# Layer 3 of a diffusion backbone: the gate product's operands without the norm's factor, and a rewritten last stage

## The chip, the cores and the metric

One core of a Trainium2 chip runs the whole program in a single launch. The metric is the device time of one execution in microseconds (us). Before the change three runs took 2101.03 us in the median (2100.48 to 2101.74).

## The reference, cut to what matters

A stack of four layers runs over 256 latent tokens and 256 context tokens of width 2048. Each layer computes RMSNorm, a shift and scale from a conditioning vector, a mixer with a SiLU gate, an output projection, and a gated residual. Layer 0 and layer 3 mix with a Fourier transform, layer 1 is an mLSTM, layer 2 is attention. In layer 3 only the latent tokens are left.

```python
shift, scale, gate = jnp.split(sc @ ada_w[i] + ada_b[i], 3, axis=-1)
hx = _rmsnorm(x, norm_g[i]) * (1.0 + scale[:, None]) + shift[:, None]
# layers 0 and 3
y = (_fourier_mix(hx) * jax.nn.silu(hx @ w_gate)) @ w_out
x = x + gate[:, None] * y
# after the last layer
return _rmsnorm(x, final_g)          # x * rsqrt(mean(x*x) + EPS) * final_g
```

RMSNorm multiplies each token by one number, rstd = 1 / sqrt(mean(x*x) + EPS). Written with a per-token rstd and a per-feature scale s = norm_g * (1 + scale), the gate product of layer 3 is hx @ w = rstd * ((x * s) @ w) + shift @ w.

## The kernel before, in words

**Layout and products.** Activations stand feature by token: a tile of 128 features by 512 tokens (256 context columns, then 256 latent columns), 16 tiles for the 2048 features, numbered kt. A product is done in fp32r in three parts: an operand x is held as h (rounded to fp32r) and l (the rest, x - h), a weight as wh and wl, and the product is h*wh + h*wl + l*wh. For each kt there are two SBUF tiles, with the tags h0 to h15 and l0 to l15, made by hl_pair (L364) and filled by split_into (L369) or modulate (L401). Each is allocated anew for each use, which waits for the readers of the tile that had the place before.

**gemm** (L276) does one group of 512 output features, in 8 steps k2 of two kt each. With orientation "A" the weights are stationary, the activation streams (columns t0 to t1), and four banks of PSUM collect 128 features each. With "B" the activation is stationary and the banks are token blocks of 128. A weight pair for one k2 comes from next_w and make_w (L258): a DMA of 512 KB into wraw (four buffers), an ACT cast to wh (L267), a DVE subtraction to wl (L268), each with three buffers. The last steps of a group, the tail (two k2 steps, if not said otherwise), run bank by bank, and done(b, ps) is called after each bank's last matmul, to take the bank out. With first=True the earlier steps run kt by kt over all the banks, otherwise bank by bank. gemm is a generator that yields every few matmuls; it yields "made" when the weights of the tail and one pair of the next group are made. run() steps it and, at given rates per yield, steps three queues of other work: fill (the mixers), bg (the conditioning) and adq.

**Order.** TensorE's (PE's) instructions run in the order in which the program emits them. For the other engines a planner sets the order, from the dependencies and its own costs: an instruction can stand earlier in an engine's queue than in the program, if what it reads is there. Where the program doesn't want that, it ties an instruction behind another.

**Conditioning.** ada (L76) holds shift, scale and gate of all layers. Their products with ada_w are made in the background by ada_dve (L212): DMA loads and DVE multiplications, 8 steps per chunk, queued in bg under the keys ga0, l1, ga1, l2, ga2, l3, ga3 (L735 to L739). bg.finish(key) runs the queue up to that key. A bias tile adab (L74) is loaded once (L615) and added in ada_finish (L164). In the first 120 us, layer 0's own conditioning is made on PE; there land_l (L180) uses the places of not yet needed l tiles as landing places, with two loads of 256 KB for a pair.

**Around the change.** out_proj (L445) is called for layer 2 at L1275: four groups "A" over 256 columns, each bank evicted by done (L458): rn = bank * gate + old residual on DVE (L467), a square on ACT (L473), its sum on DVE (L474). Then, at L1277 to L1310: bg.finish("l3"); turn_x (L1282) transposes rn into token-major xtk, on PE with ACT copies; rstd_cols (L377) sums the squares with four matmuls against ones (L383), takes the root on ACT and the reciprocal on DVE; rstd_rows (L392) spreads rstd along the tokens by two transposes of diagonals; then modulate(3, ...) makes h and l of u = x * s * rstd + shift for each kt (L406 on DVE, L407 on ACT, L408 on DVE) as gemm asks for them. gated(g) (L1300) is the gate product's group g over 256 columns; its done applies SiLU from PSUM. ahead() runs the first group up to "made". From L1352 on the four Fourier mixers are woven into the gate product's groups.

**The last stage** (L1357 to L1397) is the output projection "B" of layer 3, two banks of 128 tokens by 512 features per group. done (L1367) adds the gated bank to x for the sum of squares, and in parallel makes the final x times final_g as x*fg + bank*(gate*fg); in the last group it takes the root, scales each token block's 2048 features (1152 on DVE, 896 on ACT) and stores them with two DMAs (one from SP's queue, one from ACT's).

Of the kernel before, what the change touches and what calls it, by code (L numbers as in the profile page):

```python
# [28 lines left out]
BR1O, BR2 = 0.5, 0.25  # L29
# [20 lines left out]
def _build(tc, nc, top, A, out):  # L50
# [23 lines left out]
    adab = cp.tile([P, 4, 3, 2, KT], F32, name="adab")  # L74
# [105 lines left out]
    def land_l(kt):  # L180

        def get(src):
            raws = [hlp.tile([P, 512], F32, tag=f"l{k}", name=f"lraw{k}") for k in (kt, kt + 1)]
            for i in range(2):
                Q.dma_start(raws[i], src[:, i, :])
            return raws
        return get
# [204 lines left out]
    def rstd_rows(pp, r, nt):  # L392

        ps = bank()
        for i in range(nt):
            d = pp.tile([P, 256], F32, tag="mu", name="rdiag", bufs=2)[:, :128]
            V.tensor_scalar(d, ones, r[:, i:i + 1], None, ALU.mult)
            T.transpose(ps[:, 128 * i:128 * i + 128], d, ident)
        return ps[:, :128 * nt]
# [45 lines left out]
    def out_proj(pp, px, l, hl, old, new_dram, c0, rates, tag="xf", bufs=5, gate=None, norm=None, t0=None):  # L445
# [6 lines left out]
        for g in range(4):  # L452
# [5 lines left out]
            def done(b, ps, stream=None):  # L458
                kt = 4 * g + b
                if kt == 0 and gate:  # L460
                    gate()
                streams = range(c0 // 256, 2) if stream is None else (stream,)
                o = 256 * streams[0]
                c = slice(o - c0, o - c0 + 256 * len(streams))
                for s in streams:
                    a = 256 * s - c0
                    V.scalar_tensor_tensor(rn[:, b, a:a + 256], ps[:, 256 * s - o:256 * s - o + 256],  # L467
                                           ada[:, l, GA, s, kt:kt + 1], ro[:, b, a:a + 256], ALU.mult, ALU.add)
                if kt == 0:
                    S.activation(acc[0], rn[:, b, :], AF.Square)  # L470
                elif kt < 15:
                    sq = pp.tile([P, n], F32, tag="ys", name="sq", bufs=2)
                    S.activation(sq[:, c], rn[:, b, c], AF.Square)  # L473
                    V.tensor_tensor(acc[0][:, c], acc[0][:, c], sq[:, c], ALU.add)  # L474
                else:
                    if len(acc) == 1:
                        acc.append(pp.tile([P, n], F32, tag="sqlast", name="sqlast"))
                    S.activation(acc[1][:, c], rn[:, b, c], AF.Square)
# [106 lines left out]
    with ExitStack() as st:  # L585
# [13 lines left out]
        for j in range(4):  # L599
# [14 lines left out]
            if j == 0:  # L614
                Q.dma_start(adab, A["adab"])  # L615
                Q.dma_start(ng, A["ng"])
        for l in range(4):

            V.tensor_scalar(adab[:, l, SC], adab[:, l, SC], 1.0, None, ALU.add)
# [118 lines left out]
    bg.add("l3", ada_chain([(3, s, j, 1) for s in (SC, SH) for j in range(4)]))  # L738
# [11 lines left out]
    with ExitStack() as st:  # L750
# [10 lines left out]
        def gates():  # L761
# [7 lines left out]
            for k4 in range(4):  # L769
                for ip in range(2):  # L770
                    for q in range(4):
                        kt = 4 * k4 + q
                        T.matmul(pq[32 * q:32 * q + 32, :], gw[:, 0, 32 * kt:32 * kt + 32], hl[kt][ip].bitcast(F32),  # L773
                                 start=k4 + ip == 0, stop=k4 == 3 and ip == 1)
# [236 lines left out]
        def load_y(kt):  # L1011

            if kt < 12:
                h, l = hl_pair(kt)
                Q.dma_start(l.bitcast(F32), ytd[kt])
                S.copy(h, l.bitcast(F32))
                V.tensor_tensor(l, l.bitcast(F32), h.bitcast(F32), ALU.subtract)
# [252 lines left out]
    with ExitStack() as st:  # L1270
        pr = pool(st, "r2", reuse_waits="tile")
        bg.finish("ga2")
        with ExitStack() as st2:
            pn = pool(st2, "r2n", reuse_waits="tile")
            rn, acc = out_proj(pn, pr, 2, hl, lambda g: resid[1][:, 4 * NT * g:4 * NT * (g + 1)].rearrange(  # L1275
                "p (a b) -> p a b", a=4)[:, :, 256:512], None, 256, [(0.5, 0.12)] * 3 + [(0, 0)], bufs=6, t0=0)
            bg.finish("l3")  # L1277
# [13 lines left out]
            turns = turn_x()  # L1291
            wait = lambda: next(turns, None)
            wait()
            rc = rstd_cols(pr, acc, (0, 1), "rc2", wait)
            rrow = rstd_rows(pn, rc, 2)
            drain(turns)
            hl = Lazy(lambda kt, rn=rn, rrow=rrow, pn=pn: modulate(3, kt, rn[kt // 4][:, kt % 4, :], rrow, pn, 1, None))
            sgs, mixed3, gated3 = [], set(), set()

            def gated(g):  # L1300
                def done(b, ps):
                    if b == 0:
                        sgs.append(pr.tile([P, 4, 256], F32, tag="xf", name="sg", bufs=6))
                    S.activation(sgs[g][:, b, :], ps, AF.Silu)
# [57 lines left out]
        rf = p4.tile([P, 2], F32, name="rf")  # L1362
        for g in range(4):
            cols = slice(512 * g, 512 * g + 512)
            gf = []

            def done(b, ps):  # L1367
                if b == 0:
                    if g == 0:
                        bg.finish("row3")  # L1370
                    w = p4.tile([P, 512], F32, tag="gf", name="gf", bufs=1)
                    V.tensor_tensor(w, gate3[:, cols], fg[:, cols], ALU.mult)
                    gf.append(w)
                x = xtk[:, b, cols]
                t = p4.tile([P, 512], F32, tag="x1", name="t4", bufs=3)
                V.tensor_tensor(t, ps, gate3[:, cols], ALU.mult)
                V.tensor_tensor(t, x, t, ALU.add)
                S.activation(t, t, AF.Square, accum_out=ss4[:, b, g:g + 1])
                if g == 3:
                    r = rf[:, b:b + 1]  # L1380
                    V.tensor_reduce(r, ss4[:, b, :], AX.X, ALU.add)
                    S.activation(r, r, AF.Sqrt, bias=eps1, scale=1.0 / D)
# [5 lines left out]
                if g == 3:  # L1388
                    V.reciprocal(r, r)
                    x, o = xtk[:, b, :], out[0, 128 * b:128 * b + 128, :]  # L1390
                    V.tensor_scalar(x[:, :1152], x[:, :1152], r, None, ALU.mult)
                    S.activation(x[:, 1152:], x[:, 1152:], AF.Copy, scale=r)
                    Q.dma_start(o[:, :1152], x[:, :1152])
                    S.dma_start(o[:, 1152:], x[:, 1152:])
# [109 lines left out]
```

## Time and profile before

| | |
|---|---|
| median of three runs | 2101.03 us |
| profiled execution: its time, its span | 2097.56 us, 2095.8 us |
| DVE busy, ACT busy (shares of the span) | 75%, 40% |
| DMA: moved, mean rate | 452.60 MB, 216 GB/s |
| cast of weights, L267 ACT | 400 x 1050 ns |
| rest of weights, L268 DVE | 400 x 1223 ns |
| last matmul's start, first DMA issue of the output's last rows on ACT's queue | 2084.61, 2090.95 us |

One execution was recorded by the profiler; "profiled execution" above is that one, and its span runs from its first to its last instruction. The columns of a timeline row are the start (us from the span's start), the duration, the engine, the line of the kernel, the operation, output<-inputs by tile name, the shape and how many instructions are merged; in brackets stands how long the engine had been idle before and what ended that. The durations of matmuls overlap, since they are pipelined: the distance of two starts is the time that one takes. A chain row has the start, the time and what the program's end waited for. A row of one line gives the count, the shortest, median and longest duration in ns, and the first and last start. PE is TensorE's matmul, DVE VectorE, ACT ScalarE, SP the engine whose queue issues most DMAs.

### The profile page before, as it was taken

What the parts mean: (1) busy time and instruction counts of PE and PEld (TensorE: products, weight loads), DVE (VectorE), ACT (ScalarE), POOL (GpSimd) and SP (SyncE); (2) the same over time, 40 slices, a digit from 0 to 9 for tenths busy, and PEclk for the clock granted to TensorE, in tenths of its full rate; (3) what the DMA queues carried; (4) which work ended last, traced back from release to release, by engine and by line L of the source; (5) the groups of instructions that cost most, each with busy time, mean ns of one, the idle gap of its engine ahead of it and who ended that gap; (6) DMA issues with size and microseconds to landing.
All of it is one profiled execution on the core that took longest, in us unless ns stands there. A gap on an engine that the chain in (4) does not pass through costs nothing.

```text
span 2095.8 us, 30020 instructions
## 1 busy us (share of the span) xinstructions
PE 2056.8 (98%) x11405; PEld 1726.5 (82%) x11405; DVE 1569.3 (75%) x2921; ACT 844.9 (40%) x1414; POOL 17.5 (1%) x29
## 2 busy tenths in 40 slices
PE   7999999999999999999999999999999999999997
PEld 4678777798788888888888888888888888999986
DVE  6578888837787898799776788865657886557766
ACT  5442232226343324323432343224645555455443
POOL 0000000000000000000000000000000000000000
PEclk9999999999999999999999999999999999999999
DMA  9966878863565665577667678983343554554464
GB/s 394 347 241 204 293 249 302 322 219 98 167 195 171 221 233 179 172 255 250 207 240 282 221 238 300 339 316 102 100 143 129 165 181 138 181 191 154 164 186 151
DMA packets 127601, 452.60 MB, mean 216 GB/s; under 512 B 14400, under 2 KB 16976, under 8 KB 124640
## 3 DMA queue, kind: packets, MB, share of 16 engines
q1 hardware_dynamic: 126992, 448.71, 62.9%
q8 instruction: 89, 1.46, 0.3%
q10 hardware_dynamic: 464, 1.97, 0.3%
q14 instruction: 56, 0.46, 0.1%
HBM read 436.96 MB, written 13.67 MB: 215 GB/s over the span
## 4 chain that ended last, share of the span: by engine, by line
PE 94%; DVE 3%; ACT 1%; DMA 1%; issue 0%; SPq 0%; ACTq 0%; DVEq 0%
PE acc L309 83%; PE xb L198 2%; PE xb L904 2%; PE xb L518 1%; PE xb L1178 1%; PE xb L551 1%; PE xb L856 1%; PE xb L1163 1%; DVE wl L268 1%; PE xb L892 1%; PE xb L773 0%; PE xb L944 0%; PE xb L1149 0%; PE xb L1147 0%; PE xb L1146 0%
## 5 line engine op out<-in xcount | busy, mean ns | idle before, releaser
L268 DVE TENSOR_TENSOR wl<-wraw,wh 128x1024 fp32r<-128x1024 f32 x400 | 488.6, 1223 | 356.9 <-ACT wh L267 342.9
L267 ACT CAST wh<-wraw 128x1024 fp32r<-128x1024 f32 x400 | 419.6, 1050 | 700.9 <-PE acc L309 598.4
L309 PE MATMUL acc<-h,wh 128*128 128x512 f32 (+1 forms) x1936 | 680.5, 351 | 6.3 <-ACT h L407 3.0
L309 PE MATMUL acc<-l,wh 128*128 128x512 f32 (+1 forms) x1936 | 670.8, 346 | 1.2 <-DVE l L408 0.8
L309 PE MATMUL acc<-h,wl 128*128 128x512 f32 (+1 forms) x1936 | 669.8, 346 | 0.1
L309 PEld LDWEIGHTS acc<-h,wh 128*128 128x128 f32 x1936 | 367.1, 190 | 63.6 <-issue 11.3
L309 PEld LDWEIGHTS acc<-l,wh 128*128 128x128 f32 x1936 | 366.8, 189 | 49.3 <-DVE l L373 2.2
L309 PE MATMUL acc<-wh,h 128*128 128x512 f32 x1024 | 405.8, 396 | 1.0 <-ACT h L407 1.0
L309 PEld LDWEIGHTS acc<-h,wl 128*128 128x128 f32 x1936 | 367.3, 190 | 42.3 <-DVE wl L268 0.6
L309 PE MATMUL acc<-wh,l 128*128 128x512 f32 x1024 | 400.1, 391 | 0.0
L309 PE MATMUL acc<-wl,h 128*128 128x512 f32 x1024 | 399.5, 390 | 0.0
L228 DVE SCALAR_TENSOR_TENSOR araw<-araw,cb 128x1024 f32<-128x1024 f32 x288 | 349.3, 1220 | 8.6 <-DMA araw<-in_ada_t_dram 7.5
L309 PEld LDWEIGHTS acc<-wh,l 128*128 128x128 f32 x1024 | 192.2, 188 | 41.6 <-DVE l L408 0.4
L309 PEld LDWEIGHTS acc<-wh,h 128*128 128x128 f32 x1024 | 192.4, 188 | 40.4 <-issue 3.6
L309 PEld LDWEIGHTS acc<-wl,h 128*128 128x128 f32 x1024 | 192.5, 188 | 35.7 <-issue 0.2
L228 DVE SCALAR_TENSOR_TENSOR ajunk<-araw,cb 128x1024 f32<-128x1024 f32 x160 | 196.1, 1226 | 0.0
L198 PE MATMUL xb<-araw,cpad 128*32 128x256 f32 x696 | 49.0, 396 | 5.6 <-ACT wh L267 3.6
L473 ACT ACTIVATE sq<-rn 128x256 f32<-128x256 f32 (+1 forms) x48 | 24.7, 515 | 55.6 <-DVE rn L467 53.8
L467 DVE SCALAR_TENSOR_TENSOR rn<-acc,ada,rold 128x256 f32<-128x256 f32 x80 | 36.0, 479 | 6.8 <-PE acc L309 6.6
L198 PEld LDWEIGHTS xb<-araw,cpad 128*32 128x32 f32 x696 | 19.1, 110 | 26.2 <-DMA araw<-in_ada_p_dram 6.9
L474 DVE TENSOR_TENSOR sqacc<-sqacc,sq 128x256 f32<-128x256 f32 (+1 forms) x48 | 26.1, 544 | 4.3 <-ACT sq L473 3.7
L372 ACT CAST h<-F 128x512 fp32r<-128x512 f32 (+1 forms) x32 | 15.9, 513 | 30.5 <-PE acc L309 28.4
(274 smaller groups left out, 1695.7 us busy)
## 6 DMA issues: line engine op xcount, KB each, us to landing
araw<-in_ada_t_dram SPq DMA_DIRECT2D x288, 512.0 KB, 5.1
wraw<-in_w1in_dram SPq DMA_DIRECT2D x128, 512.0 KB, 4.4
araw<-in_ada_p_dram SPq DMA_DIRECT2D x87, 512.0 KB, 7.2
wraw<-in_w2in_dram SPq DMA_DIRECT2D x80, 512.0 KB, 3.5
wraw<-in_w0g_dram SPq DMA_DIRECT2D x32, 512.0 KB, 6.4
wraw<-in_w0o_dram SPq DMA_DIRECT2D x32, 512.0 KB, 5.9
wraw<-in_w1o_dram SPq DMA_DIRECT2D x32, 512.0 KB, 6.8
wraw<-in_w2o_dram SPq DMA_DIRECT2D x32, 512.0 KB, 3.7
```

The costliest lines, as they stand in the source:

```text
L198: T.matmul(ps[32 * q:32 * q + 32, :256], cpad[:, 4 * kq + q, :], rv[q // 2][:, 256 * (q % 2):256 * (q % 2) + 256], start=kq == 0, stop=kq ...
L228: V.scalar_tensor_tensor(o, rv, 1.0, cb[:, v + 2 - nv, part], ALU.mult, ALU.mult, accum_out=am[:, v, i, hf:hf + 1])
L267: S.copy(wh, raw)
L268: pace.append(V.tensor_tensor(wl, raw, wh.bitcast(F32), ALU.subtract).ins)
L309: T.matmul(o, lhsT, rhs, start=start, stop=stop)
L467: V.scalar_tensor_tensor(rn[:, b, a:a + 256], ps[:, 256 * s - o:256 * s - o + 256], ada[:, l, GA, s, kt:kt + 1], ro[:, b, a:a + 256], ALU. ...
L473: S.activation(sq[:, c], rn[:, b, c], AF.Square)
L474: V.tensor_tensor(acc[0][:, c], acc[0][:, c], sq[:, c], ALU.add)
L518: T.matmul(ps[:, o:o + 128], eo[:, e, s, 128 * d:128 * d + 128], cm, start=True, stop=True)
L551: T.matmul(ps[:, o:o + w], M[:, par, i, :], mv(i), start=i == 0, stop=i == 1)
L856: T.matmul(sp[:, :ns], q[:, hh, dg], k[:, 2 + hh, :ns], start=ip == 0, stop=ip == 2)
L904: T.matmul(po[:, :256], w[:, 128 * k:128 * k + 128], v[:, k, 256 * hh:256 * hh + 256], start=k + ip == 0, stop=k == nb - 1 and ip == 2)
```

## The change

It has four parts.

*The gate product of layer 3.* out_proj gets a hook "more", called after each bank's eviction in layer 2's projection. It is scaled(kt, x): one ACT copy makes h = x * s into columns 256 to 511 of the h tile that layer 2 has left there (its attention product needs those columns no more; the projection reads columns 0 to 255), one DVE instruction makes the rest l. The l3 conditioning gets one key per chunk of the scale, finished at kt = 0, 4, 8, 12, and l3s for the shift, finished behind the projection. The h and l tiles become 514 columns wide: columns 512 and 513 get the shift (split into h and rest), by 32 small copies, half of them on DVE and half on ACT. The gate product then runs over 258 columns. Its done copies the column 256, which is shift @ w, to c on ACT, multiplies the other 256 by rrow (rstd along the tokens) on DVE and applies SiLU with the bias c on ACT. The product starts at once: its steps alternate with the transposes of x, and further steps are put behind the sums of squares, the root, and the diagonals (wait). rstd_rows makes both diagonals before its transposes. The rate of bg during the projection goes from 0.12 to 0.05.

*Joint rest tiles.* The l tiles of a pair of kt become one tile of 2 x 514; land_l lands a pair with one load of 512 KB.

*adab* goes: the bias is loaded into ada itself.

*The last stage.* new_x adds the gated bank to x in place and squares x, with the sum; x is multiplied by final_g afterwards, and in the last group into t, beside the square. The two instructions for bank*(gate*fg) and the tile gf go. The last group has a tail of three k2 steps; the scaling and storing is cut into four parts (576 and 576 on DVE with SP's queue, 384 and 512 on ACT with its own).

```diff
-BR1O, BR2 = 0.5, 0.25
+BR1O, BR2, W2R = 0.5, 0.25, 0.05
...
-        V.tensor_tensor(dst, src, adab[:, l, s, v0:2, kts], ALU.add)
+        V.tensor_tensor(dst, src, dst, ALU.add)
...
     def land_l(kt):
         def get(src):
-            raws = [hlp.tile([P, 512], F32, tag=f"l{k}", name=f"lraw{k}") for k in (kt, kt + 1)]
-            for i in range(2):
-                Q.dma_start(raws[i], src[:, i, :])
-            return raws
+            raw = hlp.tile([P, 2, 512], F32, tag=f"l{kt // 2}", name=f"lraw{kt // 2}")
+            Q.dma_start(raw, src)
+            return [raw[:, 0, :], raw[:, 1, :]]
...
+    rests = {}
     def hl_pair(kt):
-        h = hlp.tile([P, 512], F32R, tag=f"h{kt}", name=f"h{kt}")
-        l = hlp.tile([P, 512], F32R, tag=f"l{kt}", name=f"l{kt}")
-        return h, l
+        h = hlp.tile([P, 514], F32R, tag=f"h{kt}", name=f"h{kt}")
+        t, had = rests.get(kt // 2, (None, (kt,)))
+        if kt in had:
+            rests[kt // 2] = t, had = hlp.tile([P, 2, 514], F32R, tag=f"l{kt // 2}", name=f"l{kt // 2}"), set()
+        had.add(kt)
+        return h, t[:, kt % 2, :]
...
+            def scaled(kt, x):
+                if kt % 4 == 0:
+                    bg.finish(f"l3{kt // 4}")
+                h, lo = hT[kt]
+                S.activation(h[:, 256:512], x, AF.Copy, scale=ada[:, 3, SC, 1, kt:kt + 1])
+                V.scalar_tensor_tensor(lo[:, 256:512], x, ada[:, 3, SC, 1, kt:kt + 1], h[:, 256:512].bitcast(F32),
+                                       ALU.mult, ALU.subtract)
...
-            turns = turn_x()
-            wait = lambda: next(turns, None)
-            wait()
-            rc = rstd_cols(pr, acc, (0, 1), "rc2", wait)
-            rrow = rstd_rows(pn, rc, 2)
-            drain(turns)
-            hl = Lazy(lambda kt, rn=rn, rrow=rrow, pn=pn: modulate(3, kt, rn[kt // 4][:, kt % 4, :], rrow, pn, 1, None))
+            bg.finish("l3s")
+            shift = p3.tile([P, 2, KT], F32R, name="shift")
+            S.copy(shift[:, 0, :], ada[:, 3, SH, 1, :])
+            V.tensor_tensor(shift[:, 1, :], ada[:, 3, SH, 1, :], shift[:, 0, :].bitcast(F32), ALU.subtract)
+            for kt in range(KT):
+                for i in range(2):
+                    (S.copy if i else V.tensor_copy)(hT[kt][i][:, 512:514],
+                                                     shift[:, i, kt:kt + 1].bitcast(F32).to_broadcast([P, 2]))
...
-                    S.activation(sgs[g][:, b, :], ps, AF.Silu)
+                    sg = sgs[g][:, b, :]
+                    c = p3.tile([P, 1], F32, tag="c3", name="c3", bufs=4)
+                    S.copy(c, ps[:, 256:257])
+                    V.tensor_tensor(sg, ps[:, 0:256], rrow, ALU.mult)
+                    S.activation(sg, sg, AF.Silu, bias=c)
...
-                return gemm(hl, "A", 256, 512, done, first=g == 0)
+                return gemm(hT, "A", 256, 514, done, first=g == 0)
...
-            first = ahead(gated(0))
+            first, turns = gated(0), turn_x()
+            def wait(n=1):
+                for _ in range(n):
+                    next(first)
+                    next(turns, None)
+            wait(4)
+            rc = rstd_cols(pr, acc, (0, 1), "rc2", lambda: wait(2))
+            wait(2)
+            rrow = p3.tile([P, 256], F32, name="rrow")
+            S.copy(rrow, rstd_rows(pn, rc, 2, lambda: wait(1)))
+            drain(turns)
...
+        def new_x(x, ps, cols, acc):
+            t = p4.tile([P, 512], F32, tag="x1", name="t4", bufs=3)
+            V.tensor_tensor(t, ps, gate3[:, cols], ALU.mult)
+            V.tensor_tensor(x, x, t, ALU.add)
+            S.activation(ps, x, AF.Square, accum_out=acc)
+            return t
+        def finish_x(b, t):
+            V.tensor_tensor(t, xtk[:, b, 1536:], fg[:, 1536:], ALU.mult)
+            r, x, o = rf[:, b:b + 1], xtk[:, b, :], out[0, 128 * b:128 * b + 128, :]
+            V.tensor_reduce(r, ss4[:, b, :], AX.X, ALU.add)
+            S.activation(r, r, AF.Sqrt, bias=eps1, scale=1.0 / D)
+            V.reciprocal(r, r)
+            for c in (slice(0, 576), slice(576, 1152)):
+                V.tensor_scalar(x[:, c], x[:, c], r, None, ALU.mult)
+                Q.dma_start(o[:, c], x[:, c])
+            for c, src in ((slice(1152, 1536), x[:, 1152:1536]), (slice(1536, 2048), t)):
+                S.activation(x[:, c], src, AF.Copy, scale=r)
+                S.dma_start(o[:, c], x[:, c])
...
-                t2 = p4.tile([P, 512], F32, tag="x1", name="t5", bufs=3)
-                V.tensor_tensor(t2, ps, gf[0], ALU.mult)
-                V.tensor_tensor(x, x, fg[:, cols], ALU.mult)
-                V.tensor_tensor(x, x, t2, ALU.add)
...
-            run(gemm(hl, "B", 256, 512, done, first=g == 0), 0, 0.25)
+            run(gemm(hl, "B", 256, 512, done, first=g == 0, tail=3 if g == 3 else 2), 0, 0.25)
```

More of the change, by code (lines that the diff above doesn't have):

```diff
@@ L73, in _build @@
     cb = cp.tile([P, 2, D], F32, name="cb")
-    adab = cp.tile([P, 4, 3, 2, KT], F32, name="adab")
     ng = cp.tile([P, 4, 2, KT], F32, name="ng")
@@ L390, in rstd_cols, with rstd_rows @@
         return r
-    def rstd_rows(pp, r, nt):
+    def rstd_rows(pp, r, nt, wait=lambda: None):
+        ds = [pp.tile([P, 256], F32, tag="mu", name="rdiag", bufs=2)[:, :128] for _ in range(nt)]
+        for i, d in enumerate(ds):
+            V.tensor_scalar(d, ones, r[:, i:i + 1], None, ALU.mult)
+        wait()
         ps = bank()
-        for i in range(nt):
-            d = pp.tile([P, 256], F32, tag="mu", name="rdiag", bufs=2)[:, :128]
-            V.tensor_scalar(d, ones, r[:, i:i + 1], None, ALU.mult)
+        for i, d in enumerate(ds):
             T.transpose(ps[:, 128 * i:128 * i + 128], d, ident)
@@ L443, in make, with out_proj @@
             return split_into(kt, u)
-    def out_proj(pp, px, l, hl, old, new_dram, c0, rates, tag="xf", bufs=5, gate=None, norm=None, t0=None):
+    def out_proj(pp, px, l, hl, old, new_dram, c0, rates, tag="xf", bufs=5, gate=None, norm=None, t0=None, more=None):
         n = 512 - c0
@@ L468, in done @@
                                            ada[:, l, GA, s, kt:kt + 1], ro[:, b, a:a + 256], ALU.mult, ALU.add)
+                if more:
+                    more(kt, rn[:, b, :])
                 if kt == 0:
@@ L614, in _build @@
             if j == 0:
-                Q.dma_start(adab, A["adab"])
+                Q.dma_start(ada, A["adab"])
                 Q.dma_start(ng, A["ng"])
         for l in range(4):
-            V.tensor_scalar(adab[:, l, SC], adab[:, l, SC], 1.0, None, ALU.add)
+            V.tensor_scalar(ada[:, l, SC], ada[:, l, SC], 1.0, None, ALU.add)
         r0 = p0.tile([P, 4], F32, name="r0")
@@ L737, in _build @@
     bg.add("ga2", ada_chain([(2, GA, j, 1) for j in range(4)]))
-    bg.add("l3", ada_chain([(3, s, j, 1) for s in (SC, SH) for j in range(4)]))
+    for j in range(4):
+        bg.add(f"l3{j}", ada_chain([(3, SC, j, 1)]))
+    bg.add("l3s", ada_chain([(3, SH, j, 1) for j in range(4)]))
     bg.add("ga3", ada_chain([(3, GA, j, 1) for j in range(4)]))
@@ L772, in gates @@
                         kt = 4 * k4 + q
[L773 removed]
+                        T.matmul(pq[32 * q:32 * q + 32, :], gw[:, 0, 32 * kt:32 * kt + 32], hl[kt][ip][:, 0:512].bitcast(F32),
                                  start=k4 + ip == 0, stop=k4 == 3 and ip == 1)
@@ L1014, in load_y @@
                 h, l = hl_pair(kt)
-                Q.dma_start(l.bitcast(F32), ytd[kt])
-                S.copy(h, l.bitcast(F32))
-                V.tensor_tensor(l, l.bitcast(F32), h.bitcast(F32), ALU.subtract)
+                hy, ly = h[:, 0:512], l[:, 0:512]
+                Q.dma_start(ly.bitcast(F32), ytd[kt])
+                S.copy(hy, ly.bitcast(F32))
+                V.tensor_tensor(ly, ly.bitcast(F32), hy.bitcast(F32), ALU.subtract)
                 last[kt] = h, l
@@ L1274, in _build @@
             pn = pool(st2, "r2n", reuse_waits="tile")
+            def scaled(kt, x):
[5 more added lines that the diff above has]
+                                       ALU.mult, ALU.subtract)
             rn, acc = out_proj(pn, pr, 2, hl, lambda g: resid[1][:, 4 * NT * g:4 * NT * (g + 1)].rearrange(
-                "p (a b) -> p a b", a=4)[:, :, 256:512], None, 256, [(0.5, 0.12)] * 3 + [(0, 0)], bufs=6, t0=0)
-            bg.finish("l3")
+                "p (a b) -> p a b", a=4)[:, :, 256:512], None, 256, [(0.5, W2R)] * 3 + [(0, 0)], bufs=6, t0=0, more=scaled)
             l2st.close()
@@ L1395, in _build @@
+                if g == 0 and b == 0:
+                    bg.finish("row3")
+                x = xtk[:, b, cols]
+                t = new_x(x, ps, cols, ss4[:, b, g:g + 1])
+                if g < 3:
+                    V.tensor_tensor(x, x, fg[:, cols], ALU.mult)
+                else:
+                    finish_x(b, t)
             if g == 3:
                 S.activation(dummy, ss4[:, 0, 2:3], AF.Sqrt)
-            run(gemm(hl, "B", 256, 512, done, first=g == 0), 0, 0.25)
+            run(gemm(hl, "B", 256, 512, done, first=g == 0, tail=3 if g == 3 else 2), 0, 0.25)
```

22 lines of the change are left out of this document (removed).

## The prediction

> **What bounds the kernel now.** I read the page first, for the engine that is the bound; then the chain that ended last in order of time, for the places where that engine isn't on it; then the timeline of PE, DVE and ACT at these places.
>
> ```profile
> span 2095.8 us, 30020 instructions
> PE 2056.8 (98%) x11405; PEld 1726.5 (82%) x11405; DVE 1569.3 (75%) x2921; ACT 844.9 (40%) x1414; POOL 17.5 (1%) x29
> ```
>
> PE is idle for 2095.8 - 2056.8 = 39.0 us in all. So the change can gain only where PE waits, at the ending, or by doing less on PE. The chain, from the last projection of layer 2 on:
>
> ```profile
> 1787.37 90.72 PE acc L309 x756
> ...
> 1903.94 1.06 ACT wh L267
> 1905.03 1.23 DVE wl L268
> ...
> 1980.65 104.36 PE acc L309 x528
> ```
>
> Layer 2's output projection runs without a gap: 90.72 / 756 = 0.120 us for a matmul of 256 columns. The last projection (384 matmuls of 512 columns, by the code 4 groups x 2 banks x 16 x 3, behind 144 of 256) has none either: (104.36 - 144 x 0.120) / 384 = 0.2268 us. Between them ACT and DVE come onto the chain twice: from 1879 to 1886, and where the two rows of 1903.94 and 1905.03 stand. The third place is the ending, from 2085 on.
>
> **The boundary of layers 2 and 3.** PE's own timeline there:
>
> ```profile
> 1879.35 1.03 PE L1287 MATMUL xb<-cst,rn 128*128 128x128 f32 x8
> 1880.22 0.61 PE L383 MATMUL xb<-cst,sqacc 128*128 128x128 f32 x4
> 1881.36 0.71 PE L383 MATMUL xb<-cst,sqlast 128*128 128x128 f32 x4 [0.53 <-ACT sqlast L478]
> 1881.91 1.91 PE L1287 MATMUL xb<-cst,rn 128*128 128x128 f32 x16
> ...
> 1886.04 0.39 PE L309 MATMUL acc<-h,wh 128*128 128x256 f32 x1 [1.13 <-ACT h L407]
> ...
> 1886.79 0.28 PE L309 MATMUL acc<-h,wh 128*128 128x256 f32 x1
> ...
> 1904.30 0.30 PE L309 MATMUL acc<-l,wh 128*128 128x256 f32 x1
> ...
> 1906.93 0.28 PE L309 MATMUL acc<-h,wh 128*128 128x256 f32 x1
> ```
>
> Starts count, since ends are modelled. The transposes of 1879.35 follow the projection's last matmul. From there to 1886.04 are 6.69 us. In them PE does 32 transposes of x (by the code 4 x 2 x 4) at 0.87 / 8 = 0.109, the first row's eight until 1880.22; 8 matmuls of L383 at 0.55 / 4 = 0.137, the second four until 1881.91; and two transposes of the diagonals: 3.5 + 1.1 + 0.2 = 4.8. So 1.9 us are idle. From 1886.04 to 1886.79 three matmuls take 0.75 instead of 0.36: 0.4 lost. From 1904.30 to 1906.93 four matmuls take 2.63 instead of 0.48: 2.15 lost, while DVE works through 16 modulations. In sum 4.4 us.
>
> The change takes all three causes away. The product no longer needs rstd, since it multiplies rstd in when the banks are taken out; its operands are written during the projection before; and its first 24 matmuls stand between the transposes, the next ones behind the sums, the root and the reciprocal. All the work of the 4.8 us stays. I count the full 4.4 as gained, if the operands are there (rivals). What it adds on PE: the gate product has 4 x 4 x 16 x 3 = 768 matmuls with 2 more columns. A column costs (0.2268 - 0.120) / 256 = 0.42 ns, so 768 x 2 x 0.42 ns = 0.64 us, all on the path. Net: 4.4 - 0.64 = 3.8 us.
>
> **The rest of that edit lies off PE.** The first question is whether the operands can wait for the conditioning, as three "finish" calls move.
>
> ```profile
> L221 SPq DMA_DIRECT2D araw<-in_ada_t_dram x288: 327/328/1130, 118.3 to 1699.0; - x144
> ```
>
> All 288 loads of that background work (36 chunks of 8, the last chunk of layer 3 among them) are issued by 1699, almost 90 us before the projection starts. The background queue is empty there: the finish calls, the split of the chunks by name and the lower rate of 0.05 cost nothing.
>
> Next, "scaled" puts one ACT and one DVE instruction per tile behind each bank's eviction. Rows at the end of the projection's first group:
>
> ```profile
> 1810.43 0.48 DVE L467 SCALAR_TENSOR_TENSOR rn<-acc,ada,rold 128x256 f32<-128x256 f32 x1
> 1810.90 2.36 DVE L268 TENSOR_TENSOR wl<-wraw,wh 128x1024 fp32r<-128x1024 f32 x2
> 1813.17 0.42 DVE L474 TENSOR_TENSOR sqacc<-sqacc,sq 128x256 f32<-128x256 f32 x1
> ```
>
> Each costs about 0.44 (the nearest rows are the 0.48 of L467 and the 0.42 of L474). The eviction of the fourth bank starts at 1810.43, so the bank ended just before. The next group has one pair of weights ready, 24 x 0.120 = 2.88 us of work, and needs the next wl at about 1813.3; the first of the two wl ends at 1810.90 + 1.2 = 1812.1. The slack is 1.2 us. The planner already puts wl ahead of the L474 that stands before it in the program, since that one waits for ACT. So I expect it to put the new instructions where they delay wl by one or two of them, 0.4 to 0.9, inside the slack: cost 0, with a bound of 3.6 us in the rivals. At the fourth bank group the gate product starts with tiles 0 to 11, which are old by then.
>
> The shift columns are 34 tiny copies, which the program has behind the projection. They depend on values that are ready before it. That the planner moves such work ahead is shown at the end of layer 1, where the tables of L1062 stand in the program behind the whole projection:
>
> ```profile
> L1062 DVE TENSOR_TENSOR tab<-rope,qkn x4: 283/285/285, 1301.6 to 1302.6; 128x128 f32<-128x128 f32 x4
> ```
>
> ```profile
> 1305.82 0.87 DVE L467 SCALAR_TENSOR_TENSOR rn<-acc,ada,rold 128x256 f32<-128x256 f32 x2
> ```
>
> They ran before that projection's evictions began. I take 0 for the copies; the other bound is a rival.
>
> In the gate product each bank gets one multiplication more on DVE (0.42 by L474) and a copy of one column on ACT. 16 x 0.42 = 6.7 us on DVE over the stage:
>
> ```profile
> 1912.00:1980.00 68.00, 68.00 (x572) 66.39 (x571) 47.60 (x129) 29.54 (x64) 0.00 (x0) 1.00 0.50 157
> ```
>
> DVE (third busy column) is free for 68.0 - 47.6 = 20.4 us of this stretch and PE never stops. Cost 0.
>
> **The joint tiles and the loads at the start.** Nine pairs of 256 KB loads become nine loads of 512 KB.
>
> ```profile
> L185 SPq DMA_DIRECT2D lraw<-in_ada_p_dram x18: 328/424/542, 49.2 to 93.0; - x18
> ```
>
> No instruction of another engine is listed as waiting for them, so I take 0. The gain is at most nine issues, 9 x 0.424 = 3.8 us; the loss, a landing that is seen later for the first half, has the same size at most. That two tiles of a pair are now freed together costs at most the 3 matmuls by which their last uses differ, several pairs of weights ahead of the next writer: 0. Dropping adab and reordering the two diagonals change no wait.
>
> **The ending.** The last bank's chain, DVE and ACT:
>
> ```profile
> 2085.03 0.69 DVE L1376 TENSOR_TENSOR t<-acc,gate 128x512 f32<-128x512 f32 x1
> 2085.64 0.15 DVE L1381 TENSOR_REDUCE rf<-ss 128x1 f32<-128x4 f32 x1
> ```
>
> ```profile
> 2087.44 0.62 ACT L1378 ACTIVATE t<-t 128x512 f32<-128x512 f32 x1
> ...
> 2088.48 0.29 ACT L1382 ACTIVATE rf<-rf,eps 128x1 f32<-128x1 f32 x1 [0.33 <-DVE rf L1381]
> 2089.88 1.04 ACT L1392 ACTIVATE xtk<-xtk,rf 128x896 f32<-128x896 f32 x1 [1.10 <-DVE rf L1389]
> 2090.95 0.34 ACTq L1394 DMA_DIRECT2D out_dram<-xtk  x1
> ```
>
> The first bank's work sits between the last bank's steps (its reduction at 2085.64 is the first such row), so the last bank's square starts only at 2087.44. In the change: t at 2085.03, x 0.61 later, the square 0.61 after that with a handover of 0.05, at 2086.3. The root ends 1.33 after the square's start (2087.44 to 2088.77, with the sum's reading and reduction between), at 2087.6; with the reciprocal the scaling starts 0.3 later, at 2087.9 instead of ACT's 2089.88. The multiplication of x by the gain runs beside the square. ACT scales the old 896 elements in two parts, so its last issue comes at 2087.9 + 1.04 + 0.1 = 2089.0, 1.9 us earlier than 2090.95. The first issue comes after 384 of ACT's 896 elements, 0.45, at 2088.35, 2.6 us earlier. The last issue has 256 KB behind it instead of 448. I take 2.2, between the two. This needs the first bank out of the way: with a tail of three pairs it ends 18 x 0.2268 = 4.1 us before the last, and the chain just worked out takes 2089.0 - 2085.0 = 4.0. Weights for the longer tail: the last pair's buffer comes free as the tail starts, it is wanted 12 x 0.2268 = 2.7 us later, and wh and wl take 1.06 + 1.23 (rows of 1903.94 and 1905.03): in time by 0.4 us.
>
> **Sum.** 3.8 + 2.2 = 6.0 us. The profiled execution took 2097.56 for its span of 2095.8, 3.5 less than the median of the runs; I take the difference over to the median: 2101.03 - 6.0 = 2095.0.
>
> **Rivals.** *The shift columns come late.* If the planner leaves the copies behind the last eviction, ACT has 17 of them ahead of the first matmul. The nearest ACT row of that size:
>
> ```profile
> 1861.75 0.20 ACT L483 ACTIVATE dummy<-sqacc 128x1 f32<-128x1 f32 x1
> ```
>
> 17 x 0.20 = 3.4 us of PE waiting, the old idle time under a new name: 2098.4. Against it speaks L1062 above; for it, that the copies share ACT with the casts there. Chance 0.12.
>
> *The evictions hold up the weights.* All four DVE additions ahead of wl, 4 x 0.44, and the wait for the last ACT part, 0.6 (an instruction of that size, taken at 0.42 too, with its handovers), make 2.4, less the slack of 1.2: 1.2 us at each of three group ends, 3.6 us: 2098.6. Against: the planner's order at 1810.90. Chance 0.12.
>
> *Odd rest tiles are read more slowly (the slower side).* A row of the joint tile has 514 elements, so the odd tile starts 2056 bytes in, 8 beyond a multiple of 16. By the code 28 groups stream these tiles through PE, with 64 matmuls each that read a rest: 1792, half of them odd, 900. Each nanosecond more costs 0.9 us. From 6.7 ns on the gain is gone, from 11.3 ns (10.2 us) the kernel is slower by 0.2%. Rows that read from an odd element (63, with 129 columns), and one with 128 columns from an even one:
>
> ```profile
> 1921.56 0.89 PE xb L551 x8
> 1922.45 0.53 PE xb L556 x4
> ...
> 1935.43 0.44 PE xb L518 x4
> ```
>
> 0.111 us against 0.110: nothing beyond the added column. Only L556, with one output row, takes 0.132; its 21 ns as a price would be 19 us: 2114. Chance 0.06. The Trainium skill speaks for this rival in kind ("SBUF — State Buffer", Specifications (TRN2)): cachelines have 16 bytes, and each step to a new line pays a penalty. By an estimate from that page a row of 512 values would touch 129 lines instead of 128, under 1% of 0.2268, some 1.6 us over 900 matmuls, and the sum would be 4.4; L551's 0.111 shows no such penalty.
>
> *The loads at the start gain.* The 3.8 us above in full: 2091.2. For it: the queue is crowded there; against: nobody waits for them. Chance 0.08.
>
> **How the numbers follow.** The forecast has 0.62, with its own range of 2093.5 to 2096.8 (the ending's bounds, the restart, half a microsecond per stage). A measurement of this kernel tells about 0.2%, 4.2 us, from no change; the line is at 2096.8. Faster: 0.60 of the forecast and 0.08, 0.68. Within: the two late-work rivals and 0.01 to 0.02, 0.25. Slower: 0.07. The range goes from the loads' gain, 2091.0, to both late-work rivals together in part, 2100.5.
>
> **What would show it.** Right: matmuls of the gate product between the transposes of the boundary, no PE wait over 0.3 us from 1787 to the last projection's end, tiny copies on DVE and ACT before or during layer 2's projection, and some 8.6 us instead of 10.8 from the last matmul to the span's end. Wrong: a PE wait on ACT or DVE copies of the shift at the boundary; waits on wl at group ends; a spacing above 0.121 in the gate product or above 0.2268 elsewhere; a changed length of the first 120 us.

## The result, and the profile after

The change makes the kernel 0.7% slower: 2115.99 us in the median of 6 runs (2114.44 to 2119.59), against 2100.85 for the kernel before beside it. The ratio is 1.0073, with a 95% interval of 1.006 to 1.0086. The forecast of 2095.0 us was wrong by 21 us, and its range ended at 2100.5.

The page of the changed kernel, its span and its engines:

```profile
span 2115.0 us, 30025 instructions
PE 2081.2 (98%) x11405; PEld 1727.3 (82%) x11405; DVE 1559.2 (74%) x2920; ACT 852.0 (40%) x1450; POOL 18.0 (1%) x29
```

PE has as many matmuls as before and is idle for 33.8 us instead of 39.0, but it is busy for 24.4 us more. So it isn't waiting that grew: the matmuls themselves take longer. That doesn't fit a local cause, so I looked at a place whose work the change leaves alone, except that its tiles have become wider. In layer 1 the chain holds three stretches of 300 matmuls of 512 columns. The first of them, in the kernel before and then in the changed one (start, time, what):

```profile
714.00 68.06 PE acc L309 x300
```

```profile
723.29 69.43 PE acc L307 x300
```

They took 68.06 / 300 = 0.2269 us each, and take 0.2314 now, over 1000 us ahead of the edited layer and with a granted clock of 0.995 and 0.997 over the whole spans and 1.00 in both stretches. The chain and PE's timeline at the edited place and at the end of the changed kernel:

```profile
1811.57 91.66 PE acc L307 x774
1903.23 0.87 PE xb L1308 x8
1904.10 0.73 PE acc L307 x6
1904.83 0.87 PE xb L1308 x8
...
1909.79 5.08 PE acc L307 x42
...
1932.94 1.06 ACT wh L265
1934.02 0.77 DVE wl L266
...
1996.54 110.00 PE acc L307 x558
```

Here the change does what it says. The gate product stands between the transposes of x, and the pauses between 1879 and 1906 are gone. But the last projection, which was 0.2268 us per matmul, has (110.00 - 174 x 0.121) / 384 = 0.2316. The copies of the shift, by engine (count, shortest, median and longest ns, first and last start):

```profile
L1318 DVE CAST h<-shift x16: 160/163/164, 1816.8 to 1817.8; 128x2 fp32r<-128x2 f32 x16
L1318 ACT CAST l<-shift x16: 187/188/192, 1816.9 to 1819.3; 128x2 fp32r<-128x2 f32 x16
```

They ran at the projection's beginning, 84 us ahead of their use. The ending's timeline, the last bank's steps:

```profile
2106.13 0.40 PE L307 MATMUL acc<-wh,l 128*128 128x512 f32 x1
2106.57 0.69 DVE L1405 TENSOR_TENSOR t<-acc,gate 128x512 f32<-128x512 f32 x1 [0.28 <-PE acc L307]
...
2108.02 0.60 ACT L1407 ACTIVATE acc<-xtk 128x512 f32<-128x512 f32 x1 [1.45 <-DVE xtk L1406]
...
2109.49 0.61 ACT L1421 ACTIVATE xtk<-xtk,rf 128x384 f32<-128x384 f32 x1 [0.23 <-DVE rf L1416]
```

The scaling starts 3.36 us after the start of the last matmul (forecast 3.3), and the span ends 8.90 us after it, where it was 11.16.

An addition over the starts of all 11405 matmuls in both traces gives the account. "Idle" is what a distance of two starts exceeds 245 ns at 512 columns, 135 at 256 or 258, and 150 or 200 at the smaller ones. The matmuls of the first two rows are those of gemm. The part in brackets goes from the first transpose of x to the last projection's first matmul of 512 columns.

| part | before, us | after, us | difference |
|---|---|---|---|
| 6479 matmuls of 512 columns | 1479.4 (228.3 ns each) | 1505.4 (232.3 ns each) | +26.0 |
| 2400 matmuls of 256 or 258 columns | 288.5 | 193.7 + 93.0 | -1.8 |
| idle of PE (of it in the stage of the gate product) | 79.2 (6.4) | 76.1 (3.2) | -3.0 (-3.2) |
| last matmul's start to the span's end | 11.16 | 8.90 | -2.3 |

With 0.4 in the other shapes this is the 19.2 us of the spans. The 26 us lie everywhere: each of gemm's six pairs of a streamed and a stationary tile has become 3.2 to 4.8 ns slower.

### The profile page after: what moved, and what is told of

Read it like the earlier page. It is cut to its first block, busy times and chain, and to the rows that moved or that the text cites. A ratio compares the mean times of both kernels' runs of the same rounds, so it can differ in the third digit from the quotient of the medians.

```text
span 2115.0 us, 30025 instructions
## 1 busy us (share of the span) xinstructions
PE 2081.2 (98%) x11405; PEld 1727.3 (82%) x11405; DVE 1559.2 (74%) x2920; ACT 852.0 (40%) x1450; POOL 18.0 (1%) x29
## 4 chain that ended last, share of the span: by engine, by line
PE 94%; DVE 3%; ACT 1%; DMA 1%; issue 1%; SPq 0%; DVEq 0%
PE acc L307 83%; PE xb L196 2%; PE xb L914 2%; PE xb L526 1%; PE xb L559 1%; PE xb L1189 1%; PE xb L866 1%; DVE wl L266 1%; PE xb L902 0%; PE xb L1174 0%; PE xb L654 0%; PE xb L245 0%; PE xb L783 0%; PE xb L954 0%; DMA araw<-in_ada_p_dram 0%
## 5 line engine op out<-in xcount | busy, mean ns | idle before, releaser
L307 PE MATMUL acc<-h,wh 128*128 128x512 f32 (+2 forms) x1936 | 684.6, 354 | 4.9 <-ACT h L376 2.7
L307 PE MATMUL acc<-l,wh 128*128 128x512 f32 (+2 forms) x1936 | 673.6, 348 | 0.4 <-DVE l L377 0.3
L307 PE MATMUL acc<-h,wl 128*128 128x512 f32 (+2 forms) x1936 | 672.9, 348 | 0.0
L196 PEld LDWEIGHTS xb<-araw,cpad 128*32 128x32 f32 x696 | 19.2, 110 | 24.6 <-issue 5.9
L447 ACT ACTIVATE mu<-mu,ada 128x256 f32<-128x256 f32 x48 | 27.0, 595 | 2.1 <-DVE mu L446 1.9
```

The lines of the kernel that those rows point to most:

```text
L196: T.matmul(ps[32 * q:32 * q + 32, :256], cpad[:, 4 * kq + q, :], rv[q // 2][:, 256 * (q % 2):256 * (q % 2) + 256], start=kq == 0, stop=kq ...
L307: T.matmul(o, lhsT, rhs, start=start, stop=stop)
L447: S.activation(u[:, c], u[:, c], AF.Identity, scale=ada[:, self.l, SC, s, kt:kt + 1], bias=ada[:, self.l, SH, s, kt:kt + 1])
```

## The experiments

The suspect is the layout of SBUF. The traces hold no addresses, so the distances here and below are worked out from the sizes of the tiles in the program. Before, every h and l tile has 512 columns (2048 bytes) and every weight tile 4096 bytes, so all of them lie a multiple of 2048 bytes apart. With 514 columns an h tile has 2056 bytes and is taken to occupy 2080 (rounded up to 32, which no run here shows), a joint l tile 4128, with its odd half at 2056. **Theory A**: a matmul's pace depends on the distance of its stationary tile from its streamed row. **Rival B**, the forecast's own: rows that start 8 bytes past a multiple of 16 are read slowly. **Rival C**: another part of the change. Later came **D**, the distances matter only beside the accesses of other engines and DMAs, and **E**, the addresses themselves matter.

**e1_pitch520.** The kernel before with tiles of 520 columns, 2080 bytes, all starts multiples of 32 bytes. (Here and in all variants of before but e10, adab is merged into ada, as in the change. In the diffs a constant stands as its number, and only the lines that matter are shown.)

```diff
-        h = hlp.tile([P, 512], F32R, tag=f"h{kt}", name=f"h{kt}")
-        l = hlp.tile([P, 512], F32R, tag=f"l{kt}", name=f"l{kt}")
+        h = hlp.tile([P, 520], F32R, tag=f"h{kt}", name=f"h{kt}")
+        l = hlp.tile([P, 520], F32R, tag=f"l{kt}", name=f"l{kt}")
```

> The kernel before with every h and l tile 520 columns wide instead of 512 (tiles start 2080 bytes apart, all on multiples of 32 bytes; the bias adab loaded into ada, as in the change), nothing else. Theory A, that a matmul's distance to the next depends on how the addresses of the streamed row and of the stationary tile stand to each other, and that the kernel before owes its even 0.2277 us to tiles that are all a multiple of 2048 bytes apart: 512-column matmuls at about 0.232 us, 6479 of them 4 ns longer, +26 us, and up to 4 us back from the 256-column ones: 2120 to 2127. Theory B, that the odd rest tiles at 8 bytes beyond a multiple of 16 are slow: no change, 2101. Theory C, that another part of the change costs the time: 2101.

Measured: 2122.32 us (ratio 1.0101, 1.0084 to 1.0117). B and C fall as the cause: there is no odd start, nothing of the change but the merged adab (which e9 below has too, at a ratio of 1.0001), and the whole loss. The same stretch of the chain:

```profile
722.90 69.65 PE acc L309 x300
```

**e2_odd514.** The kernel before with joint rest tiles of 2 x 514 columns, h tiles as they were.

```diff
-        l = hlp.tile([P, 512], F32R, tag=f"l{kt}", name=f"l{kt}")
...
+            rests[kt // 2] = t, had = hlp.tile([P, 2, 514], F32R, tag=f"l{kt // 2}", name=f"l{kt // 2}"), set()
```

> The kernel before with joint rest tiles of 2 x 514 columns (the odd one starts 8 bytes beyond a multiple of 16; the h tiles keep their 512 columns; adab loaded into ada), nothing else of the change. Theory A: only the products with l stand in a changed relation, a third of the matmuls and their neighbours: +8 to +17 us, 2109 to 2118. Theory B: the whole loss, +20 to +26 us. Theory C: no change, 2101.

Measured: 2121.45 us (1.0102, 1.0087 to 1.0117), 69.45 us for the 300 matmuls. That is more than A's 2109 to 2118 and is B's number; by its time alone this run would speak for B, which e1 has ruled out as the only cause. By the sizes, h and weights still lie a multiple of 256 bytes apart here, and all matmuls are slow none the less: those that read no rest tile (h with wh or wl) have become 3.0 to 3.9 ns slower. B says nothing of those; e12 explains it.

**e3_cols_inside.** The whole change with 512-column tiles. The shift goes into columns 254 and 255, as soon as the projection has read them, and the gate product runs over 254 to 511.

```diff
-                    (S.copy if i else V.tensor_copy)(hT[kt][i][:, 512:514],
+                    (S.copy if i else V.tensor_copy)(hT[kt][i][:, 254:256],
...
-                return gemm(hT, "A", 256, 514, done, first=g == 0)
+                return gemm(hT, "A", 254, 512, done, first=g == 0)
```

> The whole change, but with tiles of 512 columns: the shift stands in columns 254 and 255, which layer 2's projection has freed by then, and the gate product runs over columns 254 to 511. All tiles are a multiple of 2048 bytes apart again. Theories A and B: 512-column matmuls back at 0.2277 us, and the rest of the change as it shows in its own profile, -3 us of idle time and -2.3 us at the ending: 2093 to 2097. Theory C: still about 2116.

Measured: 2093.87 us (0.9968, 0.9955 to 0.9981). The layout takes all of the loss with it, and this version beats both kernels. Its chain, layer 1 and the last projection, where (108.07 - 174 x 0.1201) / 384 = 0.2270:

```profile
712.39 68.05 PE acc L307 x300
...
1972.24 108.07 PE acc L307 x558
```

**e4_wshift32.** Only the weights (and what lies behind them) move, by 32 bytes.

```diff
+    gap = pool(top, "gap")
+    skip = gap.tile([P, 8], F32, name="skip")
...
     wp = pool(top, "w")
```

> The kernel before with all weight tiles (wraw, wh, wl) moved up by 32 bytes against the activations (and adab loaded into ada); h and l are a multiple of 2048 bytes apart among themselves, and so are wh and wl. Theory A with the relation of stationary to streamed operand: the distance of two matmuls changes, by up to 4 or 5 ns, 2095 to 2127. Theory A with the relation of one streamed row to the next alone: no change, 2101. Theories B and C: no change, 2101.

Measured: 2127.29 us (1.0129, 1.0114 to 1.0144). No streamed activation tile moved against another:

```profile
722.83 69.99 PE acc L312 x300
```

So A holds. What it does not tell is which distances are good, and whether it is the distance.

**e5_sweep.** A bench with controlled distances, which leaves the model out and times matmuls alone; each block of 96 matmuls follows the other without a pause, from 81.33 us on.

```python
CONF = ((0, 0), (2, 0), (8, 0), (16, 0), (32, 0), (64, 0), (96, 0), (128, 0), (256, 0), (0, 8), (8, 8), (0, 0))
...
wh, wl = (wx[:, o + d + 128 * b:o + d + 128 * b + 128] for o in (0, 1024))
```

> A bench: the whole model is left out and zeros are stored. 104 warming matmul triples, then blocks of 96 matmuls (streamed h or h and l, stationary wh or wl in the order h wh, h wl, l wh, four banks), in each of which the stationary tiles lie d floats beyond a multiple of 2048 bytes from the streamed rows: d = 0, 2, 8, 16, 32, 64, 96, 128, 256, then only the row l moved by 8 floats, then weights and l both by 8, then 0 again; for 512 columns, and three of them for 256 columns. The sweep is run twice, first with nothing beside it, then with 128 weight loads of 512 KB, ACT casts and DVE subtractions beside it. Theory A (the distance of the stationary tile from the streamed row sets the pace; first two kinds of A): A512, only the distance modulo 512 bytes counts: 226 to 228 ns at d = 0, 128, 256, and 231 to 234 ns at the others. A2048: 226 to 228 ns at d = 0 alone, 231 to 234 ns elsewhere. Theory D (the distances matter only through what other engines and DMAs do in SBUF at the same time): one pace at all d in the first sweep, 227 against 232 in the second alone. Theory E (not the distance but the addresses themselves, or other tiles): one pace at all d in both sweeps.

Windows from one block's first matmul to the next one's (window, its length, then busy time and count of PE, PEld, DVE, ACT, POOL, clock, DMA share, GB/s): stationary tiles off by 0, 8, 32, 128, 256, 384 and 512 bytes, and l alone off by 32:

```profile
81.33:103.09 21.76, 21.76 (x97) 18.02 (x96) 0.00 (x0) 0.00 (x0) 0.00 (x0) 1.00 0.00 1
103.09:125.24 22.15, 22.15 (x98) 18.04 (x96) 0.00 (x0) 0.00 (x0) 0.00 (x0) 1.00 0.00 1
125.24:147.64 22.40, 22.40 (x97) 18.03 (x96) 0.00 (x0) 0.00 (x0) 0.00 (x0) 1.00 0.00 1
...
170.04:192.34 22.30, 22.30 (x97) 18.09 (x96) 0.00 (x0) 0.00 (x0) 0.00 (x0) 1.00 0.00 1
192.34:214.11 21.77, 21.77 (x98) 18.02 (x96) 0.00 (x0) 0.00 (x0) 0.00 (x0) 1.00 0.00 1
214.11:236.42 22.31, 22.31 (x97) 18.09 (x96) 0.00 (x0) 0.00 (x0) 0.00 (x0) 1.00 0.00 1
236.42:258.22 21.80, 21.80 (x98) 18.02 (x97) 0.00 (x0) 0.00 (x0) 0.00 (x0) 1.00 0.00 0
...
279.98:302.21 22.23, 22.23 (x97) 18.02 (x96) 0.00 (x0) 0.00 (x0) 0.00 (x0) 1.00 0.00 1
```

Over 96 matmuls: 226.7 to 227.0 ns at 0, 256 and 512 bytes (and 1024), 230.7 at 8, 232 to 233 at 32, 64, 128 and 384. Of the distances tried, the multiples of 256 bytes are the good ones, a finer count than either form of A had. Nothing else ran, so D falls; the second sweep, with the loads and casts beside it, repeats the numbers:

```profile
392.07:413.86 21.79, 21.79 (x98) 18.03 (x97) 12.26 (x10) 12.29 (x15) 0.00 (x0) 1.00 0.82 291
413.86:436.01 22.15, 22.15 (x97) 18.04 (x96) 15.61 (x13) 13.10 (x13) 0.00 (x0) 1.00 0.85 288
436.01:458.41 22.40, 22.40 (x97) 18.03 (x96) 15.03 (x13) 13.06 (x13) 0.00 (x0) 1.00 0.87 295
```

With 256 columns it goes the other way, first 0 and then 32 bytes off: 119.9 and 118.3 ns. The account has the same sign: in the changed kernel gemm's matmuls of 256 columns take 118.7 ns where they took 120.2.

```profile
346.38:357.89 11.51, 11.51 (x97) 11.50 (x96) 0.00 (x0) 0.00 (x0) 0.00 (x0) 1.00 0.01 1
357.89:369.25 11.36, 11.36 (x99) 11.36 (x97) 0.00 (x0) 0.00 (x0) 0.00 (x0) 1.00 0.01 1
```

**e6_wshift512.** e4 with `[P, 128]` in place of `[P, 8]`.

> The kernel before, with the weight tiles (and all behind them) moved up by 512 bytes instead of 32, the added bias tile adab merged into ada. A512: 227 ns for a 512-column matmul and 2098 to 2103 us, as before. A2048: 232 to 234 ns and 2120 to 2128 us, as with 32 bytes.

Measured: 2099.08 us in one run (the kernel before: 2096.89 to 2102.95). A2048 falls by the row below.

```profile
715.09 68.06 PE acc L312 x300
```

**e7_both32.** The gap of 32 bytes in front of the h, l and weight tiles.

```diff
+    gap = pool(top, "gap")
+    skip = gap.tile([P, 8], F32, name="skip")
...
     hlp = pool(top, "hl")
```

> The kernel before with h, l and weight tiles (and all behind them) moved up by 32 bytes together, adab merged into ada: every address changes by as much as in the run with 32 bytes, the distances between streamed and stationary tiles stay. Theory A: 227 ns and 2098 to 2103 us. Theory E (the addresses themselves, or their distance to the constants that stay in place): 232 to 234 ns and 2120 to 2128 us.

Measured: 2102.26 us in one run, inside the spread of the kernel before. E falls: moved alone the weights cost 26 us, moved together with h and l nothing, as the row shows.

```profile
713.68 68.06 PE acc L312 x300
```

**e12_sweep2.** A second bench without the model, for what e2 had left open: offsets of h, l, wh, wl by themselves.

```python
CONF = ((0, 0, 0, 0), (0, 0, 0, 8), (0, 0, 8, 0), (0, 8, 0, 0), (8, 0, 0, 0), (8, 8, 8, 8), (0, 0, 8, 8), (0, 0, 8, 16),
        (0, 8, 8, 8), (8, 8, 0, 8), (0, 0, 0, 0))
```

> A second bench: the model is left out and zeros are stored. Blocks of 96 matmuls of 512 columns in the order h wh, h wl, l wh, with separate offsets in floats of h, l, wh, wl from a multiple of 2048 bytes; then three blocks with one streamed row and the stationary tiles off by 0, 8 and 64 floats. The first bench had 226.7 ns with all offsets equal modulo 256 bytes, 233.3 with both weights off by 8, and 231.7 with l alone off. Theory A-own (a matmul is slow when its own streamed row and its own stationary tile are not a multiple of 256 bytes apart): wl alone off: 226.7, 233, 226.7 ns in the three places; wh alone off: 233, 226.7, 233; l alone off: 226.7, 226.7, 233. Theory A-next (the stationary tile that is loaded during a stream counts, that of the matmul behind): wl alone off: 233, 226.7, 226.7. Theory A-all (one tile off slows its neighbours too): all three places slow in each of these, by a mean of 230 to 233 ns. All four off by 8 together: 226.7 by each. One streamed row, stationary off by 8: 230 to 234; by 64: 226.7.

Windows as above: all at 0, wl alone off, l alone off, all four off together:

```profile
80.03:101.79 21.76, 21.76 (x97) 18.02 (x96) 0.00 (x0) 0.00 (x0) 0.00 (x0) 1.00 0.00 1
101.79:124.19 22.40, 22.40 (x98) 18.01 (x96) 0.00 (x0) 0.00 (x0) 0.00 (x0) 1.00 0.00 1
...
146.48:168.73 22.25, 22.25 (x98) 18.02 (x97) 0.00 (x0) 0.00 (x0) 0.00 (x0) 1.00 0.00 0
...
190.92:212.69 21.77, 21.77 (x98) 18.02 (x97) 0.00 (x0) 0.00 (x0) 0.00 (x0) 1.00 0.00 1
```

One tile off costs the whole triple: with wl alone off the three places take 239, 228 and 233 ns, with l alone off 231, 232 and 232 in the mean. A-all holds. So rest tiles alone are enough to slow everything, as in e2.

**e8_old_end, e9_joint512, e10_end_only, e11_cols_again** take the change apart, in the good layout: e3 with the old last stage; the kernel before with joint tiles of 2 x 512 and one landing load; the kernel before with the new last stage; and e3 once more. Their edits are the hunks of the diff above, with 512 for 514.

> The change with 512-column tiles and the shift in columns 254 and 255 (that run took 2093.87 us), and with the last stage of the kernel before. If the ending's part is as forecast, 2.2 us come back: 2096.1 us (2094.5 to 2097.5), and from the last matmul's start to the span's end some 11.2 us instead of 8.9. Rival (the ending is worth nothing by itself, since the reads of weights or the scheduler give it back): 2093 to 2094.5. What is left against the kernel before, 4 to 5 us, is then the boundary between layers 2 and 3 and the joint tiles.

> The kernel before with the joint rest tiles alone, at 2 x 512 columns (so that every half starts at a multiple of 2048 bytes from the other tiles), one landing load of 512 KB for a pair, and adab merged into ada. Joint tiles worth nothing, as forecast: a ratio of 0.999 to 1.001 against the kernel before. Rival of the prediction (the landing loads of the start gain 3.8 us): 0.998 and less idle of TensorE in the first 130 us, 35.4 us or so instead of 39. By theory A 227 ns in a 512-column matmul, since all tiles stay a multiple of 256 bytes apart; if the joining of the tiles itself slows the reads, 232 ns and a ratio of 1.01.

> The kernel before with the new last stage alone. As forecast, 2.2 us less: a ratio of 0.9990 (0.998 to 0.9997), and 8.9 us instead of 11.2 from the start of the last matmul to the span's end. Rival (the ending gives nothing, as the run of the change with the old ending may be read, which came within its own spread of the run with the new one): 1.000, with the time lost again ahead of the last matmul.

> The change with 512-column tiles and the shift in columns 254 and 255 once more, beside the two runs above on the same chip. Sum of the forecast's terms, 3.8 net at the boundary and 2.2 at the end, joint tiles nothing: a ratio of 0.9971; the first run of it gave 0.9968 (0.9955 to 0.9981). Rival (a third gain, from the joint tiles, is in it): 0.996 or less, and the run of the joint tiles alone shows it.

| run | median, us | ratio (interval) |
|---|---|---|
| e8: boundary and joint tiles | 2094.26 | 0.9975 (0.9965 to 0.9984) |
| e9: joint tiles | 2099.52 | 1.0001 (0.9992 to 1.001) |
| e10: ending | 2097.09 | 0.9988 (0.9979 to 0.9997) |
| e11: all | 2092.64 | 0.9964 (0.995 to 0.9979) |

Of 2100 us, e8 is worth 5.2 and e10 2.5, together 7.7; e11 has 7.6 in one. e8 missed its expectation: at 2094.26, just below the 2094.5 to 2097.5 named and so close to e3's 2093.87, its time could not show the ending; e10 does. Its timeline has the ending of the changed kernel: from the last matmul's start to the scaling are 3.35 us, and to the end of the span of 2096.4 some 9.1, where they were 11.2.

```profile
2087.31 0.39 PE L309 MATMUL acc<-wh,l 128*128 128x512 f32 x1
...
2090.66 0.95 DVE L1379 TENSOR_SCALAR xtk<-xtk,rf 128x576 f32<-128x576 f32 x2
```

e9 shows that joining the tiles costs and gains nothing beyond 0.1%, as long as the halves stay in step; so the 3.8 us that one rival of the forecast gave to the loads at the start did not come.

## Why the prediction was wrong

**The step that failed** is the part on the joint tiles and the loads, together with the sum: it priced the wider tiles at 0 and carried 0.2268 us for 512 columns and 0.120 for 256 over to the new layout. It asked who waits for a tile and how many loads it takes, and of the layout only, in a rival, whether a row starts oddly; never where the tiles lie to each other. The 512-column matmuls of gemm went from 228.3 to 232.3 ns, 26.0 us over 6479 of them. A sign of being wrong that the forecast itself had named, a spacing above 0.2268 us outside the gate product, is what the profile after shows.

**The rival on the slower side** looked at the right operation and missed the mechanism. It priced 8 bytes of odd start at 900 matmuls, about 0.9 us per nanosecond, so that 11.3 ns were needed. An odd start isn't needed for the loss (e1 has none); whether one alone, with all tiles in step, would cost anything was not tried. The price per matmul was smaller than the rival needed, 4 ns, but it was paid by all 6479 matmuls. Its evidence, L551 with 0.111 us beside 0.110, could not bear on it: those are 128 and 129 columns, and 256 columns already show the opposite sign. The forecast took 0.2268 from gemm alone, whose tiles all stood in step. The trace of before also has 112 matmuls of 512 columns that read other tiles, at L856, L1146 and L1147; by an addition as above they lie 230.6, 234.3 and 233.5 ns apart. One of them in its chain:

```profile
1705.25 0.24 PE xb L1147
```

Whether the places of their tiles are the reason isn't shown, but 0.2268 was not the price of every matmul of 512 columns.

**What was right.** The boundary, in its mechanism: the forecast counted 4.4 us of idle at three places, by the account's measure they had 4.0, and all of it is gone. But two new waits came in the gate product, 0.29 and 0.32 us behind the matmuls that start at 1936.39 and 1996.09, where the forecast had allowed none over 0.3. By the profile both end with the new DVE multiplication (L1329) that takes out a bank, which stands behind a rest of weights and other work on DVE (the rows of 1932.94 and 1934.02 above belong to the first); the forecast had put it at 0, from DVE's free time over the stage. The second one:

```profile
1996.54 0.39 PE L307 MATMUL acc<-h,wh 128*128 128x258 f32 x1 [0.17 <-DVE sg L1329]
```

Over the whole stage, to the last projection, 6.4 us of idle became 3.2, in the changed kernel and in e11 alike, a gain of 3.2. The late-work rivals did not occur: the projection runs without a gap with "scaled" beside it, at 91.66 / 774 = 0.1184 us in the changed kernel and at 0.1200 in e11 (the 16 ACT instructions take 0.50, the DVE ones 0.48, where 0.44 was taken), and the copies came early. The two extra columns cost nothing instead of 0.64 in e11, where a matmul of 258 columns takes 120.1 ns, as one of 256 does; in the changed kernel's layout it takes 121.1 beside 118.7. The joint tiles by themselves: 0 (e9). The ending: 2.26 us less after the last matmul in the profile, 2.5 (0.6 to 4.4) by e10, forecast 2.2. So what was counted is worth 7.6 us in e11 (4.4 to 10.5), forecast 6.0; its profiled execution has a span 5.2 us shorter than that of before.

## What to carry to other kernels

When a change alters the size of an SBUF tile, ask which other tiles it shifts, and who reads them together; here two more columns in one layer moved all operands of the matmuls and cost 26 us across four layers. For matmuls of 512 columns in fp32r keep the tiles that TensorE reads in turn, streamed and stationary, at distances that are multiples of 256 bytes, or find room for extra columns inside a tile that keeps its size. When a profile shows the same count, no more idle time and more busy time, compare the spacing of an untouched stretch first.

## What the runs showed of the hardware

In the benches, at 512 columns of fp32r, the spacing was 226.7 to 227.0 ns with h, l, wh and wl at equal offsets modulo 256 bytes, and 230.7 to 233.4 ns in every block where at least one differed, at a granted clock of 1.00 and with no other engine busy. The Trainium skill ("TensorE: Matmul & The Clock Gate", Step-by-step: what each phase is for) says that TensorE has two independent read ports, one for the streamed operand and one for the weights. The runs show no such independence in time: in e5 moving the stationary tiles alone by 32 bytes takes the pace of the streams from 226.7 to 233.3 ns. The Trainium skill ("SBUF — State Buffer", Specifications (TRN2)) charges for each step to a new line of 16 bytes; the bench shows another pattern, since 64 and 128 bytes, whole lines, cost more (233.3 and 232.3 ns) than 8 bytes do (230.7).

At 256 columns the offset tiles were faster, 118.3 against 119.9 ns, and 258 columns took no more than 256 in the good layout. Why either is so, and what in TensorE or SBUF makes the 256 bytes matter, stays open. The change with rows rounded up to 576 columns, a multiple of 256 bytes, was not tried.
